# Hybrid pooling and HGRN2 trunk on one core: the second rows' recurrence starts 21 ticks behind the first rows'

## The chip, the cores and the metric

The kernel runs on one core of a Trainium2 chip. A core has a matrix engine (TensorE, "PE" in the profile), a vector engine (VectorE, "DVE"), a scalar engine (ScalarE, "ACT"), a general engine (GpSimd, "POOL") and a sequencer that issues DMAs (SyncE, "SP"). ScalarE and GpSimd issue DMAs too, from their own instruction streams. Each engine works off its own instructions in a fixed order, and waits on semaphores for the others.

The metric is the device time of one execution in microseconds (us), the median over several executions. Before the change it is 2536.41 us (three executions, 2533.33 to 2537.66).

## The reference: what is computed

One layer over 2048 positions with 1024 channels, in float32. An input projection gives the channels of a pooling mixer, of a gated linear recurrence (HGRN2) and of two gates. Both branches are projected back, gated, summed and projected once more; a feed-forward network with a causal convolution follows.

```python
z = rmsnorm(x) @ w_in
u_pool, zq, zf, zi, zo, zg = split(z)                       # 4608 columns in all
ya = pool_mixer(u_pool) @ w_pa                              # windows 2, 4, 8, 16, a matrix per group
yb = hgrn2_mixer(zq, zf, zi, zo) @ w_pb                     # 4 heads of 128 channels
x  = x + (sigmoid(zg0) * ya + sigmoid(zg1) * yb) @ w_o
x  = x + conv_glu_ffn(rmsnorm(x)) ; return rmsnorm(x)
# the recurrence of one head, v = zi, gated at the end by silu(zo):
#   f_t = lb + (1 - lb) * sigmoid(zf_t) ; k_t = 1 - f_t
#   S_t = diag(f_t) S_{t-1} + k_t v_t^T ; o_t = S_t^T q_t
```

The state S goes along the positions, so the later rows of a head need the state that the earlier rows leave.

## The kernel before

**Halves and rows.** The 2048 positions are worked in two halves of 1024 (`mixer`, with `b0` = 0 and 2), and each half as two blocks of 512 positions: its first rows (block `b0`) and its second rows (block `b0 + 1`). A half goes through these stages: projection of the recurrence's input and output gate (`proj_io`), fourteen projection units (`Unit`, in the order fq0, g0, u0, fq1, g1, g2, fq2, g3, u1, g4, fq3, g5, g6, g7), the output projection of the pooling branch (`branch("pa", ...)`), that of the recurrence (`branch("pb", ...)`), `wo`, and the feed-forward network. A unit computes a pair of column tiles for both blocks at once, with seven products in place of eight (P1 to P7, into the PSUM tiles X, Z, V; the sums `u2`, `u3` are formed by VectorE, L1196 and L1200). Each product is 12 matmuls of 128x128 by 128x512, because every float32 operand is held as a high and a low part: ScalarE casts the high part (L231 for weights, L656 for activations), VectorE subtracts it to get the low part (L232, L657). A chain of `pa` or `pb` is 12 matmuls as well; `pa` has 16 chains, and so has `pb`.

**What sets the order.** The program is written as one stream of matmuls with tasks beside it. After every 6 matmuls of a projection (`MM_PER_TICK`) there is a tick; in a tick the weight stream goes one step on and each waiting task may go one step on. A scheduler then lays the instructions of each engine in one fixed order. Weights arrive by SP DMAs (`raw`, 8 buffers), and their split pairs `ops` have 6 buffers, so a cast of weights waits until the pair six places earlier has had its last matmul.

**The recurrence.** Unit fq*h* yields the forget gate and the query of head *h*. After its third product both blocks' forget gates are there, and `emit_fq` puts two entries in `queue`: head *h*, first rows and head *h*, second rows. Three `runner` tasks take entries from the head of the queue and run `hgrn_task` (L965), some 45 ticks long. It works in levels of the chunk: hh = 1 and 2 (L1066), `two_levels` for hh = 4 and hh = 16 (tiles `qm`: POOL copies of 64 columns at L1011, VectorE products at L1012 and L1015; matmuls `pl` at L1026; VectorE at L1034 to L1049 masks the result into `at` and scales `k`, `q` and `d`), and hh = 64 (L1079). Transposes of `k` follow (`kt`). Then the task waits until its state is there (`state_at`: for the second rows this is set when the first rows have issued their outputs `po`). Then come `pv` (L1109), the states (L1117), `po` (L1125 and L1127), the norm, `ot` (L1138, VectorE), its transposes `pt` (L1144, PE), `oh` (L1146, ScalarE), and `oh` is spilled to DRAM as `od` by a DMA that ScalarE issues (L956).

**After the units.** During `pa`, `halves_task` brings `od` back through SP (tile `oT`, L961), and splits it into `oTs...h` (L656, ScalarE) and `oTs...l` (L657, VectorE), which `pb` multiplies. All runners must be done, and then this task, before the program goes on to write `pb`. The pooling branch runs beside it in `pool_task`: window sums, `p` (L939, and for the very first block a correction of the first 16 columns at L941 and L942), its split `pl...h`, `pl...l`, and three matmuls into `pm` (L947 to L949).

In the program's names, `pl1_0` is tile `pl` of block 1, head 0; `pl0_0h` is the high part of the pooled tile of block 0, group 0. The changed kernel has the same instructions four lines further down (five or six from L1387 on).

Of the kernel before, what the change touches and what calls it, by code (L numbers as in the profile page):

```python
# [58 lines left out]

N_SLOTS = 77  # L60
N_RUN = 3
N_HEADS = 2
GO_AT = 3
LEAD = 5
# [17 lines left out]
def tile_trunk(  # L82
# [26 lines left out]
    def slot(name, cols=TB, dt=F32):  # L109
        return slots.tile([P, cols], dt, tag="s", name=name, padded_shape=[P, 528])  # L110
# [11 lines left out]
    class Task:  # L122
# [6 lines left out]
        def step(self):  # L129
            try:  # L130
# [2 lines left out]
                self.live = False  # L133
                tasks.remove(self)

    def tick():
        stream.advance(1)
        for t in list(tasks):
            t.wait -= 1
            if t.wait <= 0 and t.live:  # L140
                t.step()
# [5 lines left out]
    def mm(*args, **kw):  # L147
        count[1] = pe.matmul(*args, **kw)  # L148
        count[0] += 1
        if count[0] % MM_PER_TICK == 0:  # L150
            tick()
# [318 lines left out]
    def up_order():  # L470
        heads = [(0, 1), (2, 3), (4, 5)][:N_HEADS]
        res = [(m, p) for p in ("P1", "P2") for ms in heads for m in ms]
        res += [(m, p) for ms in heads for p in ("P6", "P5", "P7", "P4", "P3") for m in ms]

        rest = [(7 * m + 2 * i, m, p) for m in range(2 * N_HEADS, MF)
                for i, p in enumerate(ORDER)]
        return res + [(m, p) for _, m, p in sorted(rest)]
# [674 lines left out]
    def value(dst, a, ps):  # L1152
        if a is None:
            act.copy(dst, ps)
            return
        t, how = a
        if how == "from":
            return dve.tensor_tensor(dst, ps, t, ALU.subtract)  # L1158
        return dve.tensor_tensor(dst, t, ps, ALU.add if how == "add" else ALU.subtract)  # L1159
# [207 lines left out]
    def mixer(b0, forms, late):  # L1367
        vd = [dram.tile([P, NT, 512], F32, tag=f"vd{b0}_{hf}", name=f"vd{b0}_{hf}")
              for hf in range(2)]
        zd = [dram.tile([P, NT, 512], F32, tag=f"zd{b0}_{hf}", name=f"zd{b0}_{hf}")  # L1370
              for hf in range(2)]
        md, od, gd = {}, {}, {}
# [8 lines left out]
        queue = []  # L1381
        taken = [0]

        def runner():
            while taken[0] < 2 * HEADS:
                if queue:
                    taken[0] += 1  # L1387
                    yield from hgrn_task(*queue.pop(0))
                else:
                    yield 1  # L1390

        runners = [Task(runner()) for _ in range(N_RUN)]
        fq = {}

        def emit_fq(h):
            def emit(s, hf, a, ps):
                t = slot(f"{'fq'[s]}{b0 + hf}_{h}")
                fq[h, s, hf] = t
                if s == 0:
                    if a is None:  # L1400
                        act.activation(t, ps, AF.Sigmoid)
                    else:
                        value(t, a, ps)
                        act.activation(t, t, AF.Sigmoid)
                else:
                    g = slot(f"qs{b0 + hf}_{h}")
                    value(t, a, ps)
                    act.activation(g, t, AF.Sigmoid)  # L1408
                    pool.tensor_tensor(t, t, g, ALU.mult)  # L1409
                if (s, hf) == (0, 1):  # L1410
                    for i in range(2):
                        queue.append((b0 + i, h, fq[h, 0, i], fq[h, 1, i], vd[i], zd[i], od))
            return emit

        held = {}
# [69 lines left out]
        def branch(key, s, xs, evac, each):  # L1485
            ws = {}

            def chain(n, hf):
                m = M_ORDER[n]
                if n not in ws:  # L1490
                    each(n)
                    for m2 in M_ORDER[n : n + 3]:
                        for h in range(2):
                            gate(s, m2, h)
                    ws[n] = stream.get(key)
                w4 = ws[n]
                ps = bank(f"{key}{b0 + hf}_{m}")
                chain_t(ps, lambda k: (w4[:, 0, k * P : (k + 1) * P],
                                       w4[:, 1, k * P : (k + 1) * P]),
                        [xs[hf, k] for k in range(4)])  # L1500
                evac(m, hf, gate(s, m, hf), ps)
                if hf:
                    stream.used(1)


            for hf in range(2):
                for n in range(2):
                    chain(n, hf)
            for n in range(2, len(M_ORDER)):
                for hf in range(2):  # L1510
                    chain(n, hf)
# [27 lines left out]

        branch("pa", 0, mixed, evac_a, start_o)  # L1540
        while any(t.live for t in runners):
            for t in runners:
                if t.live:
                    t.step()
# [40 lines left out]
    def ffn(b0, forms, late):  # L1585
# [15 lines left out]
        def emit_up(m):  # L1601
# [41 lines left out]
            def emit(s, hf, a, ps):  # L1643
                h = slot(f"h{b0}_{m}_{s}_{hf}", 2 + TB)
                hs[s, hf] = h
                value(h[:, 2:], a, ps)
                first = (0, 0) if m >= 2 * N_HEADS else (1, 0)
                if (s, hf) == first:
# [172 lines left out]
    for b in range(0, SEQ // TB, 2):  # L1821
        forms, task, late = nxt
        if b:
            join(task)
        forms, task, late = mixer(b, forms, late)
        join(task)
        nxt = ffn(b, forms, late)
# [50 lines left out]
```

## Time and profile before

| | |
|---|---|
| median of three executions | 2536.41 us (2533.33 to 2537.66) |
| the profiled execution, its own time | 2532.39 us |
| its span in the trace | 2530.7 us |
| granted TensorE clock, mean | 0.999 |
| first half: `pa` ends and `pb` begins | 500.5 us |

The page of the profile gives busy time by engine, the idle time ahead of groups of instructions with what ended it, and the chain of work that ended last. The waits of one engine are listed with their total, their number and the longest. A table by windows gives each engine's busy time in chosen stretches, with the instructions in brackets. A timeline row is start, duration, engine, line, operation, and, in square brackets, the idle time before it. In groups, buffer and block numbers are left out of the names.

### The profile page before, as it was taken

To read this page: it belongs to the slowest core of one execution; us is meant where nothing else is said; L and a number is where in the kernel's file an instruction comes from. 1 tells how busy PE (TensorE), PEld (TensorE's weight loads), DVE (VectorE), ACT (ScalarE), POOL (GpSimd) and SP (SyncE) were. 2 spreads that over 40 slices of the span, in tenths; PEclk is the share of its full clock that TensorE was granted. 3 is DMA by queue.
4 is the path that set the end of the run, shared out by engine and by line. 5 is a ranking of instruction groups with operands and counts; after the bars stand their busy time and mean duration, and the time that the engine had idled before them with its cause. 6 is when DMAs were issued, how large, how long until landed. Compare 5 with 4: busy or idle time off the path is not lost.

```text
span 2530.7 us, 35649 instructions
## 1 busy us (share of the span) xinstructions
PE 2509.1 (99%) x11508; PEld 2053.6 (81%) x11508; DVE 1978.5 (78%) x3508; ACT 1176.1 (46%) x2218; POOL 753.4 (30%) x1127
## 2 busy tenths in 40 slices
PE   9999999999999999999999999999999999999998
PEld 7888888788888888888888888888888888888886
DVE  7889878598898777885596778765979888778755
ACT  6534343334555454554554343442355554445534
POOL 4344453003354334451320202200033432325410
PEclk9999999999999999999999999999999999999999
DMA  8878777777898879897344343446443454447852
GB/s 270 272 180 233 202 206 231 219 230 244 199 260 228 229 230 241 261 366 243 124 147 150 112 132 108 139 146 225 149 155 117 151 154 135 152 134 245 321 166 97
DMA packets 252332, 493.76 MB, mean 195 GB/s; under 512 B 26544, under 2 KB 43056, under 8 KB 251824
## 3 DMA queue, kind: packets, MB, share of 16 engines
q1 hardware_dynamic: 184512, 313.60, 39.1%
q0 software_dynamic: 42656, 112.74, 17.6%
q10 hardware_dynamic: 24976, 65.13, 7.6%
q8 instruction: 91, 1.49, 0.2%
q14 instruction: 97, 0.79, 0.1%
HBM read 381.79 MB, written 187.17 MB: 225 GB/s over the span
## 4 chain that ended last, share of the span: by engine, by line
PE 91%; DVE 5%; issue 1%; DMA 1%; POOL 1%; ACT 1%; SPq 0%; DVEq 0%; POOLq 0%; ACTq 0%
PE dn_P L148 16%; PE up_Z L148 14%; PE up_X L148 10%; PE up_V L148 10%; PE wo_P L148 6%; PE gr_Z L148 4%; PE pb L148 4%; PE pa L148 3%; PE io_Z L148 3%; PE gr_X L148 3%; PE fr_Z L148 2%; PE gr_V L148 2%; PE io_V L148 2%; PE fr_X L148 2%; PE fr_V L148 2%; PE pl L1026 1%
## 5 line engine op out<-in xcount | busy, mean ns | idle before, releaser
L231 ACT CAST ops<-raw 128x512 fp32r<-128x512 f32 x744 | 459.7, 620 | 817.8 <-PE dn_P L148 177.4
L232 DVE TENSOR_TENSOR ops<-raw,ops 128x512 fp32r<-128x512 f32 x744 | 553.0, 747 | 216.3 <-ACT ops L231 208.4
L1614 DVE SCALAR_TENSOR_TENSOR e<-h,cols,e 128x512 f32<-128x512 f32 x176 | 143.2, 818 | 30.9 <-ACT e L1612 26.3
L1612 ACT ACTIVATE e<-h,cols 128x512 f32<-128x512 f32 x176 | 142.3, 814 | 25.1 <-DVE h L1159 18.2
L1617 DVE SCALAR_TENSOR_TENSOR e<-h,cols,e 128x512 f32<-128x512 f32 x176 | 133.9, 770 | 2.5
L961 POOL DMA_DIRECT2D g_P<-dg_P x154 | 83.8, 545 | 160.3 <-PE dn_P L148 114.1
L1269 POOL TENSOR_TENSOR gf_P<-e,e 128x512 f32<-128x512 f32 x44 | 61.2, 1392 | 150.4 <-DVE e L1623 96.2
L1269 POOL TENSOR_TENSOR gf_P<-gf_P,e 128x512 f32<-128x512 f32 x44 | 59.1, 1344 | 72.0 <-DVE e L1623 71.5
L1409 POOL TENSOR_TENSOR q<-q,qs 128x512 f32<-128x512 f32 x16 | 21.7, 1357 | 185.2 <-ACT qs L1408 178.7
L1607 POOL COPY h<-h 128x2 f32<-128x2 f32 x88 | 40.8, 476 | 117.3 <-DVE h L1158 110.4
L1446 ACT ACTIVATE gt<-gt,cols 128x512 f32<-128x512 f32 x48 | 34.8, 725 | 86.8 <-DVE gt L1159 71.5
L1621 ACT ACTIVATE e<-e 128x512 f32<-128x512 f32 x88 | 55.6, 632 | 38.9 <-DVE e L1617 38.7
L1609 POOL COPY hist<-h 128x2 f32<-128x2 f32 x88 | 35.0, 398 | 117.6 <-DVE h L1159 115.8
L1159 DVE TENSOR_TENSOR h<-up_u,up_V 128x512 f32<-128x512 f32 x88 | 60.0, 682 | 10.2 <-PE up_V L148 9.7
L1244 DVE TENSOR_TENSOR x<-x,wo_P 128x512 f32<-128x512 f32 x88 | 56.0, 680 | 12.1 <-PE wo_P L148 11.9
L1244 DVE TENSOR_TENSOR ac<-ac,dn_P 128x512 f32<-128x512 f32 x72 | 47.1, 681 | 16.7 <-PE dn_P L148 16.5
L1011 POOL COPY qm<-q 128x64 f32<-128x64 f32 x64 | 29.9, 494 | 96.2 <-issue 25.9
L1026 PE MATMUL pl<-qm,k 128*128 128x192 f32 x256 | 50.6, 327 | 3.7 <-DVE k L1047 3.5
L1637 POOL DMA_DIRECT2D dg_P<-gf_P x88 | 50.7, 576 | 8.3 <-POOL gf_P L1269 7.4
L1607 POOL COPY h<-hist 128x2 f32<-128x2 f32 x88 | 45.0, 518 | 27.4 <-DVE m_T42l L657 27.3
L1194 ACT COPY up_e<-up_X 128x512 f32<-128x512 f32 x44 | 25.8, 586 | 58.2 <-PE up_X L148 53.1
L1026 PEld LDWEIGHTS pl<-qm,k 128*128 128x128 f32 x256 | 43.9, 189 | 9.6 <-POOL u L925 2.2
(1285 smaller groups left out, 8088.0 us busy)
## 6 DMA issues: line engine op xcount, KB each, us to landing
g_P<-dg_P POOLq DMA_DIRECT2D x154, 256.0 KB, 6.2
raw<-in_w_up_t SPq DMA_DIRECT2D x132, 256.0 KB, 3.2
raw<-in_w_in_t SPq DMA_DIRECT2D x98, 256.0 KB, 3.5
dg_P<-gf_P POOLq DMA_DIRECT2D x88, 256.0 KB, 4.0
dg_P<-e SPq DMA_DIRECT2D x66, 256.0 KB, 3.6
raw<-in_w_dn SPq DMA_DIRECT2D x66, 256.0 KB, 3.9
x<-in_x SPq DMA_DIRECT2D x64, 256.0 KB, 4.9
gd<-gt ACTq DMA_DIRECT2D x64, 256.0 KB, 3.2
```

The source lines that it names most:

```text
L148: count[1] = pe.matmul(*args, **kw)
L231: self.mark = act.copy(hi, v)
L232: low = self.low = dve.tensor_tensor(lo, v, f32(hi), ALU.subtract)
L961: eng.dma_start(t, d)
L1026: ins = pe.matmul(pa_[:, c * 192 : c * 192 + 192], ks[:, (i + c) * P : (i + c + 1) * P], mv[:, c].rearrange("p s x -> p (s x)"), start=Tru ...
L1159: return dve.tensor_tensor(dst, t, ps, ALU.add if how == "add" else ALU.subtract)
L1244: dve.tensor_tensor(t, t, ps[j], ALU.add if sg > 0 else ALU.subtract)
L1269: pin(eng.tensor_tensor(t, x0, x1, op))
L1607: pool.tensor_copy(h[:, 0:2], hist[:, mt] if hf == 0 else hs[s, 0][:, TB : TB + 2])
L1612: in_turn(act.activation(t, h[:, 2:], AF.Identity, bias=col(o_cb + mt), scale=col(o_cw + 4 * MF + mt)))
L1614: in_turn(second(dve.scalar_tensor_tensor(t, h[:, 1 : 1 + TB], col(o_cw + 2 * MF + mt), t, ALU.mult, ALU.add)))
L1617: dve.scalar_tensor_tensor(t, h[:, 0:TB], col(o_cw + mt), t, ALU.mult, ALU.add)
```

## The change

`queue` entries now carry the tick from which they may be taken. The first rows' entry carries the present tick, the second rows' entry the present tick plus 21. A runner takes the head of the queue only when its tick has come. The tick counter goes up in `tick()` and in the loop that runs the runners to their end after `pa`. In the kernel before, both entries could be taken at once, and the second rows waited for the state near their end.

```diff
+APART = 21
...
+    ticks = [0]
+
     def tick():
+        ticks[0] += 1
         stream.advance(1)
...
             while taken[0] < 2 * HEADS:
-                if queue:
+                if queue and queue[0][0] <= ticks[0]:
                     taken[0] += 1
-                    yield from hgrn_task(*queue.pop(0))
+                    yield from hgrn_task(*queue.pop(0)[1])
...
                     for i in range(2):
-                        queue.append((b0 + i, h, fq[h, 0, i], fq[h, 1, i], vd[i], zd[i], od))
+                        queue.append((ticks[0] + APART * i, (b0 + i, h, fq[h, 0, i], fq[h, 1, i],
+                                                             vd[i], zd[i], od)))
...
         while any(t.live for t in runners):
+            ticks[0] += 1
             for t in runners:
```

No instruction is added or taken away; the same work stands in another order on every engine. Three places show it.

On TensorE, in the second fq unit (`fr0_1`, tile V), before the change, head 0's `pv` is followed by the pooled product `pm0_0` and head 0's outputs:

```order
L148 MATMUL fr0_1_V_2031<-x1_T13h_781,ops52_1910 128x512
L1109 MATMUL pv0_0_2056<-v0_0_1451,kt0_0_1992 128x128 x4
L947 MATMUL pm0_0_2113<-pl0_0h_2019,ops42_1555 128x512
L1125 MATMUL po0_0_2127<-v0_0_1451,at0_0_1456 128x128
L948 MATMUL pm0_0_2113<-pl0_0l_2020,ops42_1555 128x512
```

and after the change:

```order
L152 MATMUL fr0_1_V_1969<-x1_T13h_781,ops52_1832 128x512
L1113 MATMUL pv0_0_1994<-v0_0_1451,kt0_0_1920 128x128 x4
L1030 MATMUL pl1_0_4_0_2004<-qm1_0_4_0_1941,k1_0_1768 128x192 x2
L1030 MATMUL pl1_0_4_2_2020<-qm1_0_4_2_1947,k1_0_1768 128x192 x2
L951 MATMUL pm0_0_2080<-pl0_0h_1957,ops42_1531 128x512
L1129 MATMUL po0_0_2094<-v0_0_1451,at0_0_1456 128x128
```

The second rows' level hh = 4 now stands between the first rows' `pv` and the pooled product.

On VectorE at the same place, after the change (there, before it, the split weights `ops53` to `ops55` stood ahead of `p0_0`, with nothing of the recurrence between `p0_0` and its low part `pl0_0l`):

```order
L943 SCALAR_TENSOR_TENSOR p0_0_1953<-s0_0_1_1837,u0_0_1822 128x512
L1038 COPY_PREDICATED at1_0_1771<-m4_957,pl1_0_4_0_2004 128x32x4
L1021 TENSOR_TENSOR q1_0_1364<-qm1_0_4_2_1947,f1_0_1436 128x16x8
L1050 TENSOR_TENSOR f1_0_1436<-f1_0_1436 128x32
L945 TENSOR_TENSOR p0_0_1953<-s0_0_1_1837,inv_119 128x16
L1041 COPY_PREDICATED at1_0_1771<-m33_1080,pl1_0_4_0_2004 128x16x8
L1038 COPY_PREDICATED at1_0_1771<-m4_957,pl1_0_4_2_2020 128x32x4
L1051 TENSOR_TENSOR k1_0_1768<-k1_0_1768,f1_0_1436 128x32x12
L1053 TENSOR_TENSOR f1_0_1436<-f1_0_1436 128x32
L946 TENSOR_TENSOR p0_0_1953<-p0_0_1953,u0_0_1822 128x16
```

The pooled tile `p0_0` is now finished behind two copies from `pl1_0_4_2`, the matmul tile that stands just ahead of `pm0_0` on TensorE.

On VectorE during `pa`, where `ops137` and `ops138` are weights of `wo` and `oTs0_2l` the low part of head 2's fetched first rows, before:

```order
L232 TENSOR_TENSOR ops137_5214<-raw103_4812,ops137_5214 128x512
L657 TENSOR_TENSOR oTs0_1l_5112<-oT0_1_5109,oTs0_1h_5111 128x512
L1519 TENSOR_TENSOR ya0_2_5115<-gl0_0_2_5003,pa0_2_5085 128x512
L657 TENSOR_TENSOR oTs0_2l_5127<-oT0_2_5124,oTs0_2h_5126 128x512
L232 TENSOR_TENSOR ops138_5249<-raw104_4840,ops138_5249 128x512
```

and after, where `ot1_3` (head 3's second rows, needed by the transposes `pt1_3` on TensorE) stands behind that low part:

```order
L236 TENSOR_TENSOR ops137_5214<-raw103_4767,ops137_5214 128x512
L661 TENSOR_TENSOR oTs0_1l_5098<-oT0_1_5095,oTs0_1h_5097 128x512
L1524 TENSOR_TENSOR ya0_2_5101<-gl0_0_2_4959,pa0_2_5071 128x512
L661 TENSOR_TENSOR oTs0_2l_5113<-oT0_2_5110,oTs0_2h_5112 128x512
L1142 SCALAR_TENSOR_TENSOR ot1_3_5122<-po1_3_5047,ro1_3_5062,z1_3_4996 128x128 x4
L236 TENSOR_TENSOR ops138_5249<-raw104_4804,ops138_5249 128x512
```

In the same stretch of SP's queue, the fetch `oT0_2` stood ahead of the weight load `raw111`; now it stands behind it.

On ScalarE at the end of `pa`, before, `oh1_3` and its spill `od1_3` stood twelve rows ahead of these:

```order
L656 CAST oTs1_1h_5174<-oT1_1_5172 128x512
L656 CAST oTs1_2h_5189<-oT1_2_5187 128x512
L231 CAST ops140_5328<-raw106_4940 128x512
L656 CAST oTs1_3h_5201<-oT1_3_5199 128x512
```

and after:

```order
L660 CAST oTs1_1h_5165<-oT1_1_5163 128x512
L660 CAST oTs1_2h_5180<-oT1_2_5178 128x512
L235 CAST ops140_5328<-raw106_4899 128x512
L1150 ACTIVATE oh1_3_5195<-pt1_3_5190,cols_84 128x512
L960 DMA od1_3_5197<-oh1_3_5195 128x512
L660 CAST oTs1_3h_5201<-oT1_3_5199 128x512
```

Head 3's second rows are now spilled behind the cast of `ops140`, the last tile ahead of the fetch's own cast.

## The prediction, made before the changed kernel was run

> **What bounds the kernel now.** I read the page first, for the engine that fills the span, then the waits of TensorE in the first half's recurrence stage (98 to 501 us), since only what TensorE waits for there can be won back by another order.
>
> ```profile
> span 2530.7 us, 35649 instructions
> PE 2509.1 (99%) x11508; PEld 2053.6 (81%) x11508; DVE 1978.5 (78%) x3508; ACT 1176.1 (46%) x2218; POOL 753.4 (30%) x1127
> ```
>
> TensorE is busy for 99% of the span: 2530.7 − 2509.1 leaves 21.6 us without a matmul anywhere. The change takes no matmul away, so the most it can win is a part of that. TensorE's waits in the stage, as a list (total, times, longest):
>
> ```profile
> PE pl L1026 <- DVE k L1047: 3.5, 2, 1.8
> PE pt L1144 <- DVE ot L1138: 1.8, 1, 1.8
> PE ur_Z L148 <- DVE ur_u L1196: 1.1, 1, 1.1
> PE gr_Z L148 <- DVE gr_u L1200: 0.4, 1, 0.4
> PE fr_Z L148 <- DVE fr_u L1196: 0.3, 1, 0.3
> ```
>
> All five name VectorE, and together they are 7.1 us in six waits. Two rows of the chain and of TensorE's timeline tell how much a drawn wait leaves out:
>
> ```profile
> 500.54 44.46 PE pb L148 x192
> ```
>
> ```profile
> 150.28 0.39 PE L148 MATMUL ur_V<-x_T12l,ops 128*128 128x512 f32 x1
> 150.51 0.39 PE L148 MATMUL ur_V<-x_T12h,ops 128*128 128x512 f32 x1
> ```
>
> A product really takes 44.46 / 192 = 0.2316 us of TensorE, as the starts 150.28 and 150.51 show too, but its bar is 0.39 long. A wait that follows such a bar is drawn 0.16 short. With 0.16 for six or seven places the stage loses 7.1 + 7 × 0.16 = 8.2 us. Were each place short by twice that, it would be 9.3; I keep 9.6 as the upper end. Why VectorE is late there, the table by windows says (us, then PE, PEld, DVE, ACT, POOL busy, clock, DMA share, GB/s):
>
> ```profile
> 141.00:171.00 30.00, 28.23 (x142) 23.37 (x141) 29.05 (x78) 8.41 (x17) 14.14 (x21) 1.00 0.78 175
> 245.00:271.00 26.00, 26.00 (x140) 21.65 (x139) 13.65 (x24) 9.66 (x24) 9.27 (x8) 1.00 0.60 185
> 298.00:324.00 26.00, 24.89 (x127) 20.53 (x125) 25.83 (x78) 8.43 (x17) 9.30 (x11) 1.00 0.50 169
> 324.00:348.00 24.00, 24.00 (x128) 20.36 (x129) 12.58 (x24) 6.79 (x19) 11.29 (x12) 1.00 0.58 183
> 1360.00:1540.00 180.00, 180.00 (x919) 151.33 (x918) 132.92 (x344) 75.30 (x169) 32.04 (x46) 1.00 0.40 121
> ```
>
> With both blocks of a head together VectorE is full in bursts (29.05 of 30.00, 25.83 of 26.00) and TensorE drops below its window there; right after, VectorE has half its time free (13.65 of 26.00, 12.58 of 24.00) and TensorE is full. In the second half (1360 to 1540) VectorE is at 132.92 of 180.00 and TensorE loses nothing, so nothing is to be won there.
>
> **The change part by part.**
>
> *Removed: the bursts.* With the second block 21 ticks later its levels fall into the free stretches. VectorE's work on a head is the same, spread over both kinds of window: (29.05 + 13.65) / 56 = 76%, near the 74% of the second half, which had no wait. I take all of the 8.2 us as won (bounds 0, if the bursts only move, to 9.6), and set aside 1.5 us for what is left of bursts in the new order, the size of one such wait (0 to 3.5).
>
> *Regrouped matmuls.* The smallest matmuls, 64 columns at hh = 64, now stand in separate groups for the two blocks:
>
> ```profile
> 161.78 1.15 PE L1079 MATMUL pl<-q,k 128*64 128x64 f32 x16
> 240.93 0.68 PE L1079 MATMUL pl<-q,k 128*64 128x64 f32 x8
> ```
>
> Two groups of 8 take 1.36 in place of 1.15: 0.2 us for each of 4 heads, 0.8 in all (0 to 0.8 per half; I take it once, for the first half and part of the second). The other matmuls cost the same in any grouping; they follow each other without a gap in both orders.
>
> *Head 0, first pooled product.* On TensorE the second block's two `pl` tiles of hh = 4 and then `pm0_0` now stand behind the first block's `pv`. What feeds them, in groups by line (count, busy, mean ns), and the high part of the pooled tile:
>
> ```profile
> L1011 POOL COPY qm<-q 128x64 f32<-128x64 f32 x32 | 13.4, 452 | 21.2 <-DVE gt L1159 6.1 <-DVE ops L232 4.9 <-DMA kwg5ins<-w112s 3.9
> L1012 DVE TENSOR_TENSOR qm<-q,f 128x64 f32<-128x64 f32 x32 | 9.1, 322 | 0.0
> L1015 DVE TENSOR_TENSOR qm<-qm,f 128x128 f32<-128x128 f32 x32 | 8.4, 283 | 0.1
> L1026 PE MATMUL pl<-qm,k 128*128 128x192 f32 x128 | 25.6, 329 | 3.7 <-DVE k L1047 3.5
> L1034 DVE COPY_PREDICATED at<-m,pl 128x128 f32<-128x128 uint8 x32 | 9.2, 287 | 0.0
> L1047 DVE TENSOR_TENSOR k<-k,f 128x384 f32<-128x384 f32 x16 | 10.9, 682 | 0.0
> L1049 DVE TENSOR_TENSOR f<-f 128x8 f32<-128x8 f32 x8 | 2.2, 274 | 0.0
> L942 DVE TENSOR_TENSOR p<-p,u 128x16 f32<-128x16 f32 x4 | 2.8, 707 | 0.1
> ```
>
> ```profile
> L656 ACT CAST pl_0h<-p x4: 620/622/624, 176.7 to 1438.9; 128x512 fp32r<-128x512 f32 x4
> ```
>
> First, the buffer of the second `qm` tile comes free only when `pv` is done: a POOL copy 0.45, VectorE 0.32 and 0.28, with the hand-overs some 1.2, against 2 × 0.329 = 0.66 of matmuls in between, a wait of 0.5. Then `pm0_0` stands right behind the second `pl`: after it VectorE has 0.29 (mask) + 0.68 (`k`) + 0.27 + 0.71 (the correction of `p`), then ScalarE 0.62, together 2.57 without one hand-over; with the four hand-overs between engines I take 3.0. In all 3.5 us in the first half (2.6 to 4.5, the upper end if VectorE is one more 0.7 us instruction behind). In the second half the correction (0.71, and its neighbour at L941) is not there, since it is only for the first block: 3.5 less 1.4 and less what VectorE's free time there covers, 1.3 (0.5 to 2.1). Nothing covers either: TensorE's next instructions stand behind in its own order, and all the matmuls ahead are done.
>
> *Head 2, unit g4.* The same pair of tiles costs its 0.5 again. Behind it the sums `u2` and `u3` of the unit, which TensorE's fourth product of the unit waits for, stand on VectorE behind second-block copies whose buffer `po` of the first block frees:
>
> ```profile
> L1200 DVE TENSOR_TENSOR gr_u<-gr_Z,gr_e 128x512 f32<-128x512 f32 x8 | 5.5, 684 | 0.0
> ```
>
> A POOL copy (0.45) and this sum (0.68) behind the end of `po` are 1.1, and a late `u2` adds some 0.3: 1.9 in the first half (0.5 to 2.5). In the second, VectorE has no backlog, which leaves 0.8 (0 to 1.9).
>
> *Head 3's `pt` during `pa`.* `ot1_3` now stands on VectorE behind the low part of fetch `oT0_2`, and this fetch on SP behind `raw111`, which needs the buffer that the weights `ops137` leave. In the trace of before that place reads (VectorE, SP; then groups and landings, us):
>
> ```profile
> 484.53 0.69 DVE L232 TENSOR_TENSOR ops<-raw,ops 128x512 fp32r<-128x512 f32 x1 [3.28 <-ACT ops L231]
> ```
>
> ```profile
> 485.25 0.33 SPq L197 DMA_DIRECT2D raw<-in_w_o  x1
> 485.64 0.42 SPq L961 DMA_DIRECT2D oT<-od  x1
> ```
>
> ```profile
> L1138 DVE SCALAR_TENSOR_TENSOR ot<-po,ro,z 128x128 f32<-128x128 f32 x32 | 9.0, 342 | 0.1
> ```
>
> ```profile
> od<-oh ACTq DMA_DIRECT2D x16, 256.0 KB, 3.9
> oT<-od SPq DMA_DIRECT2D x16, 256.0 KB, 4.1
> ```
>
> ```profile
> DMA to landing us min/median/max: 3.3/4.1/5.8
> ```
>
> VectorE's 0.69 ends at 485.22, SP issues the weight load at 485.25 and the fetch at 485.64, which by the median lands 4.1 later, at 489.7; ScalarE's high part 0.62, VectorE's low part 0.69 and the first `ot` 0.34 bring `ot1_3` to 491.4. The cast behind the row at 484.53 could start when chain `pa1_2` ended, no later than 484.53 − 0.62 = 483.9, and TensorE has 24 products of the next two chains ahead of `pt`: 483.8 + 24 × 0.2316 = 489.4. So TensorE waits 2.0 us. The shortest landing (3.3) gives 1.2, the longest (5.8) 3.7. Both halves have this place: 4.0 (2.4 to 7.4).
>
> *Between `pa` and `pb`.* The last spill `od1_3` now stands on ScalarE behind the cast of `ops140`, which waits for the buffer of the last `pa` weights, so for the last `pa` product. ScalarE in the trace of before, the end of `pa`, and the `oh` group:
>
> ```profile
> 500.80 0.62 ACT L656 CAST oTs_2h<-oT 128x512 fp32r<-128x512 f32 x1 [4.64 <-DMA oT<-od]
> 501.33 0.61 ACT L231 CAST ops<-raw 128x512 fp32r<-128x512 f32 x1
> 501.85 0.62 ACT L656 CAST oTs_3h<-oT 128x512 fp32r<-128x512 f32 x1
> ```
>
> ```profile
> 471.36 0.69 ACT L1146 ACTIVATE oh<-pt,cols 128x512 f32<-128x512 f32 x1 [5.41 <-PE pt L1144]
> ```
>
> In before `oh` was done at 472.05, 28 us ahead of `pb` (500.54). Now it takes the place behind 501.33: it starts at 501.86 and ends at 502.55, the spill lands 3.9 later at 506.45, the fetch 4.1 later at 510.55, and the high part is cast by 511.17. `pb` gets along without it for 24 products of first rows and 9 of second: 500.54 + 33 × 0.2316 = 508.18. That is 3.0 us; the low part, 0.69 more on VectorE, is needed one product later (0.45), and the PSUM bank that VectorE frees behind it adds 0.2: 3.6 per half, 7.2 in both. By the shortest landings, 2.0 of a spill (below) and 3.3, it is 0.9 per half; by 9.0 and 5.8 it is 10.
>
> ```profile
> DMA to landing us min/median/max: 2.0/4.1/9.0
> ```
>
> [...]
>
> *The sum.* 3.5 + 1.3 (head 0) + 1.9 + 0.8 (head 2) + 4.0 (`pt`) + 7.2 (`pa` to `pb`) + 0.8 (regrouping) + 1.5 (rest of bursts) = 21.0 us added; 8.2 removed: +12.8. The span becomes 2530.7 + 12.8 = 2543.5. The profiled execution took 2532.39, 4.0 under the median 2536.41, so the changed kernel's like execution would be 2545.2 and the median 2549.2; I say 2549.
>
> **The rivals.** Differences under 0.2% (5.1 us) cannot be told from none.
>
> *Faster.* Evening out VectorE is the whole effect, and the new waits are small: −8.2 + 0.8 gives 2529. For it speaks that all six waits of before are VectorE's; against it, that the places above follow from the order itself and from durations, whichever state VectorE's load is in. It decides only where the new waits are under 3 us together, so both halves' `pt` and `pb` places, 11.2 us at the medians, would have to be nearly free. That needs the spill at 2 us and the fetch under 3.3, which no fetch of before was.
>
> *No measurable change.* The transfers land at their shortest (2.0 and 3.3): `pb` costs 1.8 and `pt` 2.4 in both halves, the rest 9.8, and 9.6 come off: +4.4, 2541. [...]
>
> *Much slower.* The bursts do not go but move, since three runners now overlap one head's second rows with the next head's first rows: nothing of the 8.2 is won and the longest landings count in one half: 12.8 + 8.2 + 7 = +28, 2564.
>
> *Nothing moves.* Excluded by the order: every engine's row changes.
>
> **How the numbers follow.** The sum as worked out, between about +5 and +20, 0.63; faster, by over 0.2%, 0.10 (and nothing below 2529); no measurable change 0.16 with all of its kinds; much slower 0.11. The time is that of the likeliest, 2549. For the range I leave out the faster case and the upper half of the much slower one: 2536 to 2563. Faster 0.10, same 0.16, slower 0.74.
>
> **What would show it.** The first-half windows 141 to 171 and 298 to 324 should show TensorE full and VectorE near 76%; the waits of `pl` on `k` (3.5) and of `pt` on `ot` (1.8) there should go. New rows in TensorE's waits: `pm` on the cast `pl_0h` (3 us), `pt` on `ot` during `pa` (2 us, twice), and `pb` on `oTs_3h` or on the fetch `oT` (3 us, twice), with `oh` behind a cast at about 502. I am wrong if the last two are absent, which the landings would decide, or if `pl` still waits on `k`.

## The result, and the profile after

The changed kernel takes 2563.07 us (median of four executions, 2561.94 to 2563.83), the kernel before 2535.69 beside it (now the median of four executions, 2533.33 to 2537.66). The ratio is 1.011, with a 95% interval of 1.0098 to 1.0123: slower by about 27 us. The profiled execution took 2563.83 us with a span of 2562.1, so the two traces differ by 2562.1 − 2530.7 = 31.4 us, and this is what has to be found.

The page of the changed kernel:

```profile
span 2562.1 us, 35620 instructions
PE 2519.7 (98%) x11508; PEld 2060.3 (80%) x11508; DVE 1978.8 (77%) x3508; ACT 1177.1 (46%) x2218; POOL 729.5 (28%) x1127
```

The matmuls are the same in number, yet TensorE's busy time is 2519.7 in place of 2509.1: some matmuls took longer. The idle part of the span grew from 21.6 to 42.4. TensorE's waits in the first half's recurrence, `pa` and `pb` stages (98 to 545 us; total, times, longest):

```profile
PE pt L1148 <- DVE ot L1142: 6.2, 1, 6.2
PE fr_Z L152 <- DVE fr_u L1204: 5.1, 1, 5.1
PE pl L1070 <- DVE q L989: 3.5, 3, 1.7
PE gr_Z L152 <- DVE gr_u L1200: 2.4, 2, 1.6
PE gr_Z L152 <- DVE gr_u L1204: 2.3, 1, 2.3
PE pm L951 <- ACT pl_0h L660: 2.0, 1, 2.0
PE fr_Z L152 <- DVE fr_u L1200: 1.6, 1, 1.6
PE pl L1030 <- DVE qm L1019: 0.8, 2, 0.4
PE pb L152 <- DVE oTs_3l L661: 0.2, 1, 0.2
PE pb L152 <- ACT oTs_3h L660: 0.2, 1, 0.2
```

and in the second half's (1300 to 1800 us), where before there was none:

```profile
PE pt L1148 <- DVE ot L1142: 1.5, 1, 1.5
PE pb L152 <- ACT oTs_3h L660: 1.4, 1, 1.4
PE gr_Z L152 <- DVE gr_u L1204: 1.1, 1, 1.1
PE pm L951 <- ACT pl_0h L660: 0.6, 1, 0.6
PE pb L152 <- DVE oTs_3l L661: 0.2, 1, 0.2
```

These are 24.3 + 4.8 = 29.1 us against 7.1 before, 22.0 more. There are 19 of them in place of 6, and at 0.16 that a wait is drawn short this adds 13 × 0.16 = 2.1. The rest shows in TensorE's granted clock. The same view by windows as for the kernel before (us, PE, PEld, DVE, ACT, POOL busy, clock, DMA share, GB/s):

```profile
141.00:171.00 30.00, 30.00 (x150) 24.92 (x149) 28.18 (x59) 10.22 (x20) 13.88 (x19) 1.00 0.76 183
192.00:198.00 6.00, 5.70 (x14) 4.75 (x15) 3.08 (x13) 2.58 (x11) 2.65 (x3) 0.50 0.07 25
298.00:324.00 26.00, 26.00 (x135) 22.29 (x134) 22.40 (x58) 10.56 (x27) 9.20 (x13) 1.00 0.65 205
511.00:515.00 4.00, 3.86 (x10) 3.09 (x11) 2.65 (x7) 0.13 (x1) 0.00 (x0) 0.50 0.27 81
```

From 192 to 198 and from 511 to 515 us the clock is 0.50. TensorE's timeline at the second of these, start and duration first:

```profile
511.14 0.47 PE L1148 MATMUL pt<-ident,ot 128*128 128x128 f32 x1 [6.21 <-DVE ot L1142]
511.26 0.77 PE L152 MATMUL pa<-mxs_0h,ops 128*128 128x512 f32 x1
511.83 0.63 PE L152 MATMUL pa<-mxs_0l,ops 128*128 128x512 f32 x1
512.26 0.63 PE L152 MATMUL pa<-mxs_0h,ops 128*128 128x512 f32 x1
...
515.67 0.48 PE L152 MATMUL pa<-mxs_3l,ops 128*128 128x512 f32 x1
516.00 0.39 PE L152 MATMUL pa<-mxs_3h,ops 128*128 128x512 f32 x1
```

Behind the wait of 6.2 us the products start 0.43 us apart, until at 516.00, where a bar is 0.39 long again, the 0.23 of the kernel before is back. Four such stretches stand in the trace, at 192.9 (5.5 us), 358.9 (3.4), 511.8 (3.8) and 1789.1 (3.0), each behind a wait; no matmul of the trace of before stands in such a stretch. Together they are 15.7 us, of which 1 − 0.2316 / 0.427 = 46% is lost: 7.2 us. The account then reads 22.0 (waits) + 2.1 (drawn short) + 7.2 (half clock) = 31.3 of the 31.4. That it closes so well is partly chance: from the first product of the first unit to the first of `wo`, the two halves take 25.2 and 8.4 us longer than before, 33.6 together, and the rest of the span came out 2.1 shorter. Some 2 us of the two halves stay unassigned.

What the change was forecast to take away did go: TensorE is full from 141 to 171 (30.00 of 30.00; 28.23 before) and from 298 to 324 (26.00 of 26.00; 24.89 before), and the waits of `pl` on `k` and of `ur_Z` are no longer in the list. But VectorE was forecast near 76% there, and it is still at 28.18 of 30.00 (94%) and 22.40 of 26.00 (86%). The waits went without the evening out that was to remove them.

Two long waits have DMA landings behind them. Ahead of `fr_Z` on VectorE, and its store:

```profile
190.48 0.69 DVE L938 TENSOR_TENSOR s<-s 128x512 f32<-128x512 f32 x1 [5.57 <-DMA kwfq1ins<-w56s]
...
191.56 0.68 DVE L1204 TENSOR_TENSOR fr_u<-fr_Z,fr_e 128x512 f32<-128x512 f32 x1
```

```profile
kwfq1ins<-w56s SPq DMA_DIRECT2D x1, 256.0 KB, 8.7
```

A window sum of the pooling branch (L938) takes over the buffer of the weight tile `w56s`, whose copy to DRAM took 8.7 us; `fr_u`, for which TensorE waits, stands behind it in VectorE's order. Ahead of `pt`, on VectorE, on SP and on GpSimd:

```profile
510.12 0.69 DVE L661 TENSOR_TENSOR oTs_2l<-oT,oTs_2h 128x512 fp32r<-128x512 f32 x1 [8.11 <-ACT oTs_2h L660]
510.73 1.12 DVE L1142 SCALAR_TENSOR_TENSOR ot<-po,ro,z 128x128 f32<-128x128 f32 x4
```

```profile
501.28 2.06 SPq L965 DMA_DIRECT2D oT<-od  x2
```

```profile
495.33 1.01 POOL L695 TENSOR_TENSOR ro<-ro,neghalf 128x4 f32<-128x4 f32 x1
496.29 1.24 POOL L308 DMA_DIRECT2D su2s<-in_w_up_t  x1
```

The chain is the one that was forecast, but the fetch issued at 501.28 landed after 8.2 us. At 496.29, right behind the norm of head 3's second rows in GpSimd's queue, a transfer began that sums feed-forward weights in DRAM (`su2s`); it landed at 509.3. Before the change the same norm and the same transfer stood at 457 and 458 us, well ahead of the fetches.

At the end of `pa`, ScalarE:

```profile
525.27 0.61 ACT L235 CAST ops<-raw 128x512 fp32r<-128x512 f32 x1
525.79 0.68 ACT L1150 ACTIVATE oh<-pt,cols 128x512 f32<-128x512 f32 x1
526.50 0.34 ACTq L960 DMA_DIRECT2D od<-oh  x1
532.22 0.62 ACT L660 CAST oTs_3h<-oT 128x512 fp32r<-128x512 f32 x1 [5.75 <-DMA oT<-od]
```

`oh` stands behind the cast as forecast, but the spill landed in 2.1 and the fetch in 3.5 us (2.2 and 2.8 in the second half), near or under the shortest of before (2.0 and 3.3), and `pb` waited 0.4 and 1.6 in place of 3.6.

### The profile page after: what moved, and what is told of

Same layout as the page of the kernel before. It is cut to its first block, busy times and chain, and to the rows that moved or that the text cites. A ratio compares the mean times of both kernels' runs of the same rounds, so it can differ in the third digit from the quotient of the medians.

```text
span 2562.1 us, 35620 instructions
## 1 busy us (share of the span) xinstructions
PE 2519.7 (98%) x11508; PEld 2060.3 (80%) x11508; DVE 1978.8 (77%) x3508; ACT 1177.1 (46%) x2218; POOL 729.5 (28%) x1127
## 4 chain that ended last, share of the span: by engine, by line
PE 93%; DVE 3%; DMA 2%; ACT 1%; issue 1%; POOL 0%; SPq 0%; ACTq 0%; DVEq 0%; POOLq 0%
PE dn_P L152 16%; PE up_Z L152 14%; PE up_X L152 10%; PE up_V L152 10%; PE wo_P L152 6%; PE gr_Z L152 5%; PE gr_V L152 3%; PE gr_X L152 3%; PE pb L152 3%; PE io_Z L152 3%; PE fr_Z L152 2%; PE pa L152 2%; PE io_V L152 2%; PE fr_X L152 2%; PE fr_V L152 2%; PE pl L1030 1%
## 5 line engine op out<-in xcount | busy, mean ns | idle before, releaser
L1015 POOL COPY qm<-q 128x64 f32<-128x64 f32 x64 | 20.6, 335 | 204.2 <-DVE q L1047 57.3
L1413 POOL TENSOR_TENSOR q<-q,qs 128x512 f32<-128x512 f32 x16 | 21.6, 1348 | 163.0 <-ACT qs L1412 163.0
L1248 DVE TENSOR_TENSOR x<-x,wo_P 128x512 f32<-128x512 f32 x88 | 55.5, 679 | 12.9 <-PE wo_P L152 12.8
```

The lines of the kernel that those rows point to most:

```text
L1248: dve.tensor_tensor(t, t, ps[j], ALU.add if sg > 0 else ALU.subtract)
```

## The experiments

The theory to test: the loss is made of separate places at which a producer of TensorE now comes late, two of them made long by a transfer that collides with GpSimd's sums, and of the half clock that follows TensorE's standing still. The rivals: one cause that runs through the whole program; long transfers that are long by themselves; and slow matmuls for another reason than the wait.

**One half at a time.** The delay in the first half alone, and in the second alone:

```diff
-                        queue.append((ticks[0] + APART * i, (
+                        queue.append((ticks[0] + APART * i * (b0 == 0), (
```

(for the second half, `b0 != 0`).

> The second rows begin 21 ticks later in the first half alone. Theory (many separate late producers, each where the new order puts it): by start spacing the changed kernel lost 25.7 us more than before in the first half's projection, pa and pb stages and 8.0 more in the second's, while the rest of the span came out 2.5 shorter; so 2536 + 23 to 26 = 2559 to 2562 here. Rival (one cause that runs through the whole program, such as fuller DMA queues): both halves share it and this kernel stands about midway, near 2550.

> The delay in the second half alone. Theory: 2536 + 8 = 2544, with TensorE waiting in the second half at four places (pooled product 1.3, unit g4 1.4, pt 1.7, pb 2 and a stretch at half clock 1.9) and nowhere new in the first. Rival (one cause through the whole program): near 2550.

The first half alone took 2556.51 us, the second alone 2543.34, with the kernel before at 2533.98 beside them: 22.5 and 9.4 more (ratios 1.0084, 1.0068 to 1.0101, and 1.0035, 1.0023 to 1.0046). The sum, 31.9, agrees with the 27 of the change within the intervals, and the halves are unequal, so a cause that both share equally falls. The second half's part is as the theory put it, the first half's a little under.

**One group of heads at a time.** Heads 0 to 2, and head 3 alone:

```diff
-                        queue.append((ticks[0] + APART * i, (
+                        queue.append((ticks[0] + APART * i * (h < 3), (
```

(for the other, `h == 3`).

> Head 3's second rows begin with its first rows again, in both halves; heads 0 to 2 keep the delay. Theory: the places of head 3 go (pt 6.7 and 1.7, pb 0.9 and 2.0, stretches at half clock 2.0 and 1.9, together 15 us, against 2.1 that the kernel before lost at its own pt): about 2563 - 13 = 2550. Rival (the loss at pt comes from the delay of the other heads, by the backlog that they leave): the pt wait stays and the time is above 2558.

> Only head 3 keeps the delay. Theory: 2536 + 13 = 2549, with the waits of pt and pb and the half-clock stretches behind them. If the forecast was right about places and only the transfers were slower than taken, this is the part that shows it: it had 4.0 + 7.2 = 11 us for it, less the 1.8 at pt before. Rival: the head alone finds a free SP queue and free DMA engines, pt waits 2 us and pb 3, and the time is near 2543.

Heads 0 to 2 took 2557.92 (ratio 1.0092, 1.0077 to 1.0108), head 3 alone 2540.45 (1.0026, 1.0017 to 1.0036): 23.9 and 6.5 above before. The two add up within the intervals, but my split between them was wrong: I had put 13 on head 3, and its time is nearer to the rival's 2543 than to the 2549 of the theory. With heads 0 to 2 delayed, the waits in the first half read

```profile
PE fr_Z L152 <- DVE fr_u L1204: 6.5, 1, 6.5
...
PE pt L1148 <- DVE ot L1142: 2.4, 2, 1.8
```

and head 3 alone has

```profile
PE pt L1148 <- DVE ot L1142: 5.0, 1, 5.0
```

So the `pt` wait does go with head 3's delay, and the rival for it falls. With heads 0 to 2 delayed, what head 3 no longer lost in the first half came back elsewhere: TensorE's waits there are 24.0 us in all, against 24.3. The wait of `fr_Z` alone, in an order that up to that place is the changed kernel's, is 6.5 in place of 5.1, because the same store took longer:

```profile
kwfq1ins<-w56s SPq DMA_DIRECT2D x1, 256.0 KB, 10.2
```

Behind `pb`, head 3 alone waited 0.2 in the first half, and the rival's 3 is not there either.

**Two of the sums left out.** This kernel leaves out the two colliding transfers, so its feed-forward network has other weights; on every engine all other instructions stand as in the changed kernel.

```diff
-                if add:
+                if add and (self.name, g, dst) in (("su", 0, "s3"), ("su", 2, "s2")):
+                    pass
+                elif add:
```

> Leaves out two of the transfers with which GpSimd sums feed-forward weights in DRAM (the second addend of s3 of group 0 and of s2 of group 2), so the feed-forward network gets other weights; every other instruction stands where it stood in the changed kernel. One ran from 181 to 194 us, beside the store of w56 that landed after 8.7 us; the other from 496 to 509 us, beside the fetch of head 2's first rows that landed after 8.2 us. Theory (these transfers stretch the two landings): the store lands near 5.4 and the fetch near 4.1, the wait before fr0_1's Z falls from 5.1 to about 2, that of pt from 6.2 to about 2, both half-clock stretches behind them go (2.6 and 2.0): 2563 - 12 = 2551. Rival (the landings are long by themselves, or by the weight loads beside them): nothing moves, 2562 to 2564.

2555.47 us against 2533.16 of before (1.0083, 1.0068 to 1.0098), 7.6 less than the changed kernel. The store and the two waits:

```profile
kwfq1ins<-w56s SPq DMA_DIRECT2D x1, 256.0 KB, 4.8
```

```profile
PE fr_Z L152 <- DVE fr_u L1206: 2.3, 1, 2.3
PE pt L1150 <- DVE ot L1144: 1.7, 1, 1.7
```

The store falls from 8.7 to 4.8 us and the fetch from 8.2 to 3.6; the waits fall from 5.1 to 2.3 and from 6.2 to 1.7, and the half-clock stretches behind both are gone. That these transfers stretched the landings is shown. The whole gain is less than the 12 expected, because other places moved: a wait of `pl` on `q` grew from 1.7 to 2.9 us, with a half-clock stretch behind it at 209, and the stretch behind the wait of 2.35 us in unit g4 became longer, 5.1 us in place of 3.4.

**The sum issued earlier.** The same cause taken away with all work kept: the pause of the sums begins three products later, so that `su2s` stands ahead of the norm.

```diff
-                if n == len(PROJ) - 1 and p == "P1":
+                if n == len(PROJ) - 1 and p == "P7":
                     quiet[0] = True
+                if n == len(PROJ) - 1 and p == "P1":
                     mtask = Task(pa_task())
```

> The changed kernel, but the sums of feed-forward weights pause three products later in the last unit, so that the transfer for s2 of group 2 stands ahead of the norm of head 3's second rows in GpSimd's queue, not behind it. Everything is computed. Theory (that transfer, released by the norm at 496 us, stretched the fetch in front of pt): it runs before pa's fetches, the fetch lands near 4, pt waits some 2 us and no half-clock stretch follows, 2563 - 6 = 2557. Rival (other loads keep the fetch long, or the transfer collides elsewhere): 2561 to 2564.

2561.14 us (2556.71 to 2564.58; 1.0103, 1.0085 to 1.0121), not to be told from the changed kernel. The trace shows why: the transfer ran at 444 us, the fetch landed in 3.6 and `pt` waited 1.5 as expected, but the units' order shifted a little and a new wait of 2.4 us stands at 460,

```profile
PE gr_Z L152 <- DVE gr_u L1204: 4.7, 2, 2.4
```

(2.3 in one place before), with a half-clock stretch of 3.0 us behind it. The mechanism is confirmed, the gain was given back.

**TensorE kept busy.** Transposes without a use ahead of `pt`:

```diff
+        if (b, h) == (1, 3):
+            warm(40, count[1])
         pt = bank(f"pt{b}_{h}")
```

> 40 transposes of the identity into a spare PSUM bank are put on TensorE ahead of the transposes pt of head 3's second rows in the first half; their result is not used. At 0.11 us each they fill some 4.4 of the 6.2 us that TensorE waits there. Theory (a wait of some microseconds lowers the granted clock, which then stays at 0.50 for a stretch): the starts behind pt stand 0.23 apart in place of 0.43, and the time is 2.0 us shorter, 2561. Rival A (the 0.43 spacing comes from the operands, or from contention in memory): the spacing stays and the time too, 2563. Rival B (the wait is not a wait for VectorE but for TensorE's own queue): the transposes add their 4.4, 2567.

```profile
509.01 4.53 PE L686 MATMUL warm<-ident 128*128 128x128 f32 x40
513.73 1.10 PE L1150 MATMUL pt<-ident,ot 128*128 128x128 f32 x4 [0.19 <-DVE ot L1142]
514.59 0.48 PE L152 MATMUL pa<-mxs_0h,ops 128*128 128x512 f32 x1
514.91 0.39 PE L152 MATMUL pa<-mxs_0l,ops 128*128 128x512 f32 x1
```

With TensorE busy through the wait, the same products behind it start 0.23 apart. So at this place the slow products come from TensorE's standing still, and not from their operands or from memory. The time is 2560.42, 2.6 less than the changed kernel's median, where 2.0 was expected; the interval of the ratio (1.0084 to 1.0117) does not separate it from 1.011, so the trace carries this, not the time.

**Both places kept busy.** In addition 32 transposes ahead of the Z products of unit fq1:

```diff
             for p in ORDER:
+                if (b0, n, p) == (0, 3, "P4"):
+                    warm(32, count[1])
                 u.multiply(p, forms, late)
```

> As pe_kept_busy, and 32 more transposes of the identity (some 3.6 us) on TensorE ahead of fr0_1's Z products, where it waited 5 to 6 us behind 187 us and then ran 9 products at 0.43 us. Theory (the half clock follows from TensorE standing still): that stretch of 5.5 us goes too and half of it is won, 2560.4 - 2.7 = 2557.7, with the wait itself shorter by what the transposes fill. Rival (the stretch has another cause): it stays, 2560 to 2561.

2558.28 us (1.0093, 1.0078 to 1.0108). The stretch did not go but became shorter, 3.4 us in place of 5.5: the store landed after 9.8 us here, and behind the transposes TensorE still stood still for

```profile
194.50 0.50 PE L152 MATMUL fr_Z<-x_T40h,ops 128*128 128x512 f32 x1 [2.66 <-DVE fr_u L1206]
```

So here a drop followed a wait of 2.66 us. The time is near the forecast, but the expectation that the stretch goes was missed.

**Other delays.** APART = 3, 7, 14 and 28, nothing else changed.

> APART = 3. Theory (single late producers, no law in the delay): the tasks run almost in step as before, VectorE's bursts and their 9.6 us stay, and each place that lands badly adds 2 to 5 us: 2536 to 2550. Rival (a small shift already evens VectorE out): 2526 to 2533.

> APART = 7 in place of 21. Theory (the loss is made of single late producers in an order laid without knowing them): no steady law in APART; the bursts are nearly those of before, the head 3 tail is 14 ticks shorter and od1_3 is spilled well ahead of pb: 2536 to 2545. Rival (the longer the delay, the more even VectorE and the less TensorE waits, and only the tail of head 3 costs): 2530 to 2536.

> APART = 14 in place of 21. Theory (single late producers): between 2540 and 2560, with waits at other places than with 21. Rival (evening out wins, the tail costs): less than with 21 by the whole tail, 13 us, and by a smaller backlog: 2540 or under.

> APART = 28. Theory (no law in the delay): between 2545 and 2570, with waits at other places than with 21, and head 3's second rows later still, so that pb's wait for the last spill grows by some 2 us in each half. Rival (the loss grows with the delay, 11 at 14 and 29 at 21): 2580.

| APART | time, us | before beside it | ratio, 95% interval |
|---|---|---|---|
| 3 | 2546.05 | 2534.25 | 1.0043 (1.0029 to 1.0058) |
| 7 | 2555.33 | 2533.16 | 1.0080 (1.0065 to 1.0095) |
| 14 | 2544.62 | 2533.16 | 1.0041 (1.0026 to 1.0056) |
| 21 | 2563.07 | 2535.69 | 1.0110 (1.0098 to 1.0123) |
| 28 | 2586.96 | 2534.25 | 1.0201 (1.0184 to 1.0217) |

Every delay is slower than none, and the loss does not grow evenly: 14 is better than 7. The waits that cost most are at other places each time. With 7 they are those for VectorE's sums of the u units, with 28 those for VectorE's products `qm` ahead of `pl`:

```profile
PE ur_Z L152 <- DVE ur_u L1204: 5.0, 2, 2.9
```

```profile
PE pl L1030 <- DVE qm L1019: 10.1, 3, 3.8
```

The rivals for 3, 7 and 14 fall: none is faster, and 14 is 2544.62. But the theory missed two of its own ranges: 7 came 10 above 2536 to 2545, and 28 came 17 above 2545 to 2570, nearer to the rival's 2580, so that towards 28 the loss does grow with the delay. With 28, `pb` does not wait in either half, where its wait was expected to grow by some 2 us in each. The half-clock stretches make such places dearer than their waits: five of them with 7, seven with 28 in the first half.

No kernel tried here beats the one before.

## Why the prediction was right or wrong

The direction was right, and the size was off: +12.8 us were forecast for the span, 31.4 came. Term by term, in drawn waits:

| term of the sum | forecast, us | measured |
|---|---|---|
| removed waits | −8.2 | gone, as forecast (7.1 drawn) |
| head 0, `pm0_0`, first / second half | 3.5 / 1.3 | 2.0 + 0.4 / 0.6 |
| head 2, unit g4, first / second half | 1.9 / 0.8 | 0.4 + 1.6 + 2.3 / 1.1 |
| `pt` in `pa`, first / second half | 2.0 / 2.0 | 6.2 / 1.5 |
| `pa` to `pb`, first / second half | 3.6 / 3.6 | 0.4 / 1.6 |
| regrouping | 0.8 | not separated |
| rest of bursts | 1.5 | 11.0 in six waits |
| TensorE's clock | no term | 7.2 |

**Right:** the places. All four that the order had shown are in the list of waits, in both halves, with the releasers that were named, and the six waits of before are gone. The reason given for that was not borne out: VectorE did not come near 76% (94% and 86%, above), and with it at 94% TensorE lost nothing from 141 to 171. VectorE's share of busy time did not tell where TensorE waits; at the places looked at here, what stands ahead of the producer in VectorE's row did.

**The step that failed first: "rest of bursts, 1.5".** Six waits outside the named places cost 11.0 us: 5.1 before `fr_Z`, 3.5 in three waits of `pl` on `q` (L989), 1.6 before another `fr_Z` and 0.8 before a `gr_Z`. The prediction went through the places where a moved matmul now stands ahead of its producer, and not through VectorE's row for the sums `u2` and `u3`, which TensorE needs in each unit, and for the queries `q` of a head's first level; other work now stands ahead of them. For the 5.1 before `fr_Z` the row was a window sum that waits for a buffer, so no price from VectorE's durations could have shown it.

**"`pt`, 2.0": the landing.** The chain was right, and with the colliding transfer taken away it came out at 1.7 and 1.5, but the prediction took the median landing of a fetch. The change moved the norm of head 3's second rows 38 us later in GpSimd's queue (457 to 495), and with it the sum transfer that stands behind it, onto the fetches. The prediction looked at SP's and ScalarE's queues there and left GpSimd's out.

**"`pa` to `pb`, 3.6": the landing, the other way.** Spill and fetch took 5.6 us together in the first half and 5.0 in the second, where 8.0 were taken from the medians of before; at `pt`, with a sum transfer beside it, the one fetch took 8.2. The 0.2 for a PSUM bank was the author's estimate, and the changed kernel's lists have no such wait at `pb`.

**"Head 0, 3.5".** The hand-overs in this term were an estimate of about 0.1 us each. At `pm0_0` ScalarE's cast began 0.11 us after VectorE's last correction of `p`, and the matmul 0.05 after the cast. That correction ran 0.16 us, where the group's mean of 0.71 had been taken.

**"Head 2, 1.9".** Only the last copy and the sum were priced (1.1). On VectorE a window sum (0.70 us) and two `qm` products (1.26) stood ahead of `u3` as well, and `u2` came 1.6 late in place of 0.3.

**The clock had no term.** No matmul of before ran at half clock, the longest wait in these stages was 1.8 us, and the prediction did not ask what its own forecast waits of 3 us would do. In the changed kernel the clock was 0.50 for 3.0 to 5.5 us at four places, and the products there started 0.43 us apart in place of 0.23. The runs show no length of wait that settles it: the clock fell behind single waits of 2.35 us (at 358 in the changed kernel) and 2.66 (with both places kept busy), and in four of the kernels tried behind one of 2.0 (below). Nor does each such wait cost: the same wait of 2.35 was not followed by a drop with heads 0 to 2 delayed. So the 7.2 us could not have been priced from the lengths of the waits alone, and part of it may be chance.

The rival that came nearest in time, "much slower, 2564", did so by other terms than it named: it kept the 8.2 us of the old waits and took the longest landings of before, while here the old waits went, new ones stood elsewhere, and the clock cost 7.2. That its time comes so near is luck.

## What to carry to other kernels

When a stage is at 99% of the bounding engine, a new order can win only the listed waits (here 8 us in 2536), and each place where one producer comes late can cost as much (at `pt` 6.2 us, and 1.7 more at half clock behind it). Price such a place with what stands ahead of the producer in its own queue, with the transfers that the change sets free beside it on other queues (here one fetch took 8.2 us, and 3.6 without the sum transfer), and with the clock behind the wait (here 0.50 for 3.0 to 5.5 us at four places). A change that only shifts work in time should be tried at several shifts: here 3 to 28 ticks gave 11 to 53 us not in order of the shift, since each shift made other collisions.

## What the runs showed of the hardware that was not expected

- TensorE's granted clock went to 0.50 behind some of its waits, and the products then started 0.43 apart, in the changed kernel for 3.0 to 5.5 us. Filling the wait at `pt` with transposes without a use left the products behind it 0.23 apart.
- The length of a wait did not settle whether a drop followed. In seven kernels with the delay of 21 in the first half, TensorE's matmuls stand in the same order up to 188 us, and the same wait of 2.0 us stands ahead of `pm` near 179. Behind it the clock was 1.00 in three (the changed kernel, the sums left out, the sum issued earlier) and 0.50 in four (the first half alone, heads 0 to 2, and both kernels kept busy). The changed kernel and the first half alone:

```profile
179.50:181.50 2.00, 2.00 (x12) 1.68 (x12) 1.82 (x4) 0.55 (x2) 1.88 (x2) 1.00 0.00 0
179.50:181.50 2.00, 2.00 (x9) 1.81 (x9) 1.06 (x2) 0.14 (x1) 1.46 (x2) 0.50 0.00 0
```

  Waits of 3.3 us (with APART = 3, at 157) and 3.2 (with 14, at 156) passed at 1.00, and in the second half of the changed kernel 1.4 and 0.2 us close together were followed by a drop. What else decides is not shown, so a microsecond or two between two such kernels can be chance.
- Two sum transfers of GpSimd's queue, each 13 us long, stretched a 256 KB transfer beside them from 3.6 to 8.2 us and another from 4.8 to 8.7. In six kernels with the delay of 21 in the first half that store took between 7.8 and 10.9 us, so a wait behind it varies by some 3 us between kernels that are alike up to there. A sum transfer beside it is not enough by itself: with APART = 14 the same store, issued 0.5 us after one that ran until 197, landed after 3.5 us, while a fetch issued another 0.5 us later took 13.0.
